# A seventh seven-product pair and a half piece per chunk in a hybrid encoder layer, with late keys and values parked in DRAM

## The chip, the cores and the metric

One core of one Trainium2 chip runs the kernel. Its engines each work through a queue of their own: TensorE (matmuls and weight loads), VectorE (elementwise), ScalarE (activations and copies), GpSimd, and SyncE, which issues the DMAs here. The metric is the device time of one execution in microseconds; the lower the better. The kernel before takes 1543.43 us, the median of three runs (1542.38 to 1543.45).

## The reference, cut to what matters

All data are float32. One layer on 256 tokens and 4096 features:

```python
h = layer_norm(x, emb_ln_g, emb_ln_b)              # (256, 4096)
p = h @ w_in                                       # w_in (4096, 13312)
c_b, c_c, c_h, c_z = four slices of 2048 columns   # convolution branch
a_q (2048), a_k (512), a_v (512), a_z (2048)       # attention: 16 query, 4 kv heads of 128
y_conv = c_b * conv3(c_c * c_h, conv_w) * silu(c_z)
y_attn = window_attention(a_q, a_k, a_v, sink) * silu(a_z)   # +-128 tokens, ALiBi, sink logit
y = concat(y_conv, y_attn) @ w_out                 # w_out (4096, 4096)
out = layer_norm(2 ** 0.25 * h + y, ln_g, ln_b)
```

Nearly all arithmetic is in the two matrix products, and nearly all bytes are their weights.

## The kernel before

**Tiling.** The 256 tokens are two blocks of 128 rows; the 4096 input features are 32 k-tiles of 128. The columns of w_in are cut into 26 chunks of 512, taken in the order of IN_ORDER: K, V, then AZ and Q alternately for four groups of four heads (AZ0, Q0, ... Q3), then CC, CH, CZ, CB four times (CC0 ... CB3). The output product follows in nine chunks.

**Split products.** Each float32 operand is used as a high and a low part, x = xh + xl and w = wh + wl, and each product as three matmuls: xh wh, xh wl, xl wh. xT holds the normalised input, turned, in both parts. The weights come from DRAM by SyncE into a raw buffer; ScalarE writes the high part (split_hi, L197), VectorE subtracts it for the low part (split_lo, L201).

**Steps.** The work is a written-out list of steps. A whole piece ("s" in ORDERS) is four k-tiles of a chunk, 1 MB, 24 matmuls of 512 columns (mm). A pair ("S") is two k-tiles, 512 KB, computed as a 2 x 2 block product (two halves of the tokens, two halves of the columns) with seven block products instead of eight: 21 matmuls of 256 columns (mm_pair). It needs sums of weight blocks (sums, L178 to L180, three VectorE operations that widen the 1024 loaded columns to 1792 to be split) and sums of input blocks, made once for each pair of k-tiles and kept in SC for all chunks (x_sums). x_sums also replaces a part of xT, so it runs after the last plain use of these k-tiles, which is in chunk V. K and V have eight whole pieces; the other 24 chunks have six pairs and five whole pieces. The pairs' results are gathered in PSUM in two more banks and put together by pair_copy and pair_sums (L649 to L652) and added by whole (L657).

**Order of the work.** The program order is the order of issue on each engine. Step j of the loop issues its matmuls, then split_hi of step j+3, then what `later` holds for j (the attention and convolution work, put at fixed distances from a chunk's end by `at`), then the loads that have a free buffer, then

```python
        loads(j)
        sums(j + 4)
        split_lo(j + 3)
```

The high and low parts have three buffers each, the raw weights three to six (w0 to w2, and w6 to w8 where memory is free). With four or more raw buffers a load is issued once the low part of the step that used the buffer, at most j+2, is issued; SyncE waits for it. During CC0's second half, CH0 and the start of CZ0 there are three.

**What `later` holds.** A chunk's end (chunk_end) is at the first step of the next chunk. After Q, the list SPREAD gives for four heads scores, s_add, exps, recip, norms, p_tr, p_lo, pv and out_z over 23 steps. After CH the product c * h is at the second step from there (L662), conv_tr at the fourth and fifth, conv_mul at the fifth and seventh; after CB the product with the gate, gate_tr and gate_mul at the same places. After AZ and CZ a SiLU is at the first step (z_act L504, s_act L691). In the first chunk's shadow K is turned into kT for four key heads (k_turn) and at V's end v is split (end_v); both stay in SBUF until the attention is done. y_load, y_hi and y_lo bring the finished branch outputs back as input of the output product during CB3 and the first output chunk.

Of the kernel before, what the change touches and what calls it, by code (L numbers as in the profile page):

```python
# [89 lines left out]
ALL_PAIRS = [u[1:] for u in IN_STEPS + OUT_STEPS if u[0] in ("pair", "opair")]  # L90
# [4 lines left out]
def encoder_kernel(ctx: ExitStack, tc: tile.TileContext, x, emb_g, emb_b, wi, ws, conv_w, sink, wo, ln_g, ln_b, out):  # L95
# [38 lines left out]
    def load(j, to=None):  # L134
# [47 lines left out]
    def part(j, t):  # L182
# [3 lines left out]
        return t[:, HW:] if is_pair(j) else t  # L186
# [38 lines left out]
    def mm(j):  # L225
# [4 lines left out]
        for k in range(PK):  # L230
            kt = q * PK + k
# [12 lines left out]
    def mm_pair(j):  # L244
# [10 lines left out]
        sc = lambda n: (SC[:, p, 0, n, :], SC[:, p, 1, n, :])  # L255
# [228 lines left out]
    kT = pa.tile([P, NG, 2, S], F32R, name="kT")  # L484
    v = pa.tile([P, 2, 2, W], F32R, name="v")
# [38 lines left out]
    def scores(h):  # L524
        g, a = h // GROUP, h % 2
# [565 lines left out]
```

## Time and profile before

| | us |
|---|---|
| median of three runs | 1543.43 |
| lowest, highest | 1542.38, 1543.45 |
| profiled execution | 1543.44 |
| its span in the profile | 1541.7 |
| TensorE busy with matmuls | 1525.8 |
| TensorE's weight loads, beside them | 1325.1 |
| VectorE busy | 1271.7 |
| ScalarE busy | 756.1 |

The span is from the first to the last instruction of the profiled execution; the time is that of the whole execution. Busy times of different engines overlap. The granted TensorE clock is at its full level in all 40 slices of the page. The DMAs moved 313.5 MB, 203 GB/s in the mean.

### The profile page before, as it was taken

The page shows a single profiled execution, that of the slowest core. Times are in us where ns is not written, and L with a number is a line of the kernel's source. Part 1 is how long each engine was busy: PE and PEld are TensorE (multiplying, and loading weights), DVE is VectorE, ACT ScalarE, POOL GpSimd, SP SyncE. Part 2 cuts the span into 40 slices and gives each one's busy share as a digit, 9 for nine tenths or more (in the row PEclk, how much of TensorE's full clock was granted, in tenths as well). Part 3 has the DMA queues.
Part 4 walks back from the last instruction along what each step waited for, and adds up shares of the span by engine and source line. Part 5 has one row for each costly group of instructions (what it writes and reads, how often), then busy time and mean ns, then how long its engine had stood idle before and what let it go on. Part 6 is the DMA issues. An engine that isn't in the chain of part 4 may idle for free.

```text
span 1541.7 us, 21128 instructions
## 1 busy us (share of the span) xinstructions
PE 1525.8 (99%) x8654; PEld 1325.1 (86%) x8654; DVE 1271.7 (82%) x1441; ACT 756.1 (49%) x640; POOL 1.3 (0%) x7
## 2 busy tenths in 40 slices
PE   7999999999999999999999999999999999999998
PEld 4888888888888888888888888888888888888897
DVE  7778798888897888898888889888888688888656
ACT  4545556556465554544544445444455444444331
POOL 0000000000000000000000000000000000000000
PEclk9999999999999999999999999999999999999999
DMA  7635554545545456656555655556557756666753
GB/s 283 223 138 203 205 191 169 196 175 182 203 158 188 164 188 238 217 191 208 194 199 191 219 205 186 187 208 218 192 188 274 276 185 225 253 203 235 252 182 140
DMA packets 67392, 313.51 MB, mean 203 GB/s; under 512 B 8064, under 2 KB 12128, under 8 KB 43488
## 3 DMA queue, kind: packets, MB, share of 16 engines
q1 hardware_dynamic: 66288, 310.33, 56.5%
q10 hardware_dynamic: 1008, 1.84, 0.3%
q8 instruction: 68, 1.11, 0.3%
q14 instruction: 28, 0.23, 0.0%
HBM read 304.19 MB, written 7.86 MB: 202 GB/s over the span
## 4 chain that ended last, share of the span: by engine, by line
PE 93%; DVE 3%; issue 2%; ACT 2%; DMA 0%; SPq 0%; ACTq 0%
PE acc L238 15%; PE acc L240 15%; PE acc L239 15%; PE acc L879 7%; PE acc L881 7%; PE acc L880 7%; PE pacc L263 5%; PE pacc L262 5%; PE pacc L264 4%; PE acc L263 3%; PE acc L262 3%; PE acc L264 3%; DVE wlo L201 1%; ACT whi L197 1%; PE att L476 1%
## 5 line engine op out<-in xcount | busy, mean ns | idle before, releaser
L197 ACT ACTIVATE whi<-w 128x2048 fp32r<-128x2048 f32 (+1 forms) x330 | 600.0, 1818 | 671.1 <-PE acc L240 292.3
L201 DVE TENSOR_TENSOR wlo<-w,whi 128x2048 fp32r<-128x2048 f32 (+1 forms) x330 | 712.1, 2164 | 200.1 <-ACT whi L197 198.3
L238 PE MATMUL acc<-whi,xT 128*128 128x512 f32 x1072 | 424.5, 396 | 0.0
L240 PE MATMUL acc<-whi,xT 128*128 128x512 f32 x1072 | 420.1, 392 | 0.0
L239 PE MATMUL acc<-wlo,xT 128*128 128x512 f32 x1072 | 417.4, 389 | 0.7 <-DVE wlo L201 0.7
L240 PEld LDWEIGHTS acc<-whi,xT 128*128 128x128 f32 x1072 | 201.3, 188 | 47.0
L239 PEld LDWEIGHTS acc<-wlo,xT 128*128 128x128 f32 x1072 | 201.3, 188 | 41.6 <-DVE wlo L201 1.0
L238 PEld LDWEIGHTS acc<-whi,xT 128*128 128x128 f32 x1072 | 201.5, 188 | 37.5
L879 PE MATMUL acc<-whi,xT 128*128 128x512 f32 (+1 forms) x496 | 182.9, 369 | 0.0
L881 PE MATMUL acc<-whi,xT 128*128 128x512 f32 (+1 forms) x496 | 181.8, 366 | 0.0
L880 PE MATMUL acc<-wlo,xT 128*128 128x512 f32 (+1 forms) x496 | 180.5, 364 | 0.0
L178 DVE TENSOR_TENSOR w<-w 128x512 f32<-128x512 f32 x154 | 105.2, 683 | 4.5 <-DMA w<-in_ws 4.5
L881 PEld LDWEIGHTS acc<-whi,xT 128*128 128x128 f32 x496 | 93.0, 188 | 16.9
L880 PEld LDWEIGHTS acc<-wlo,xT 128*128 128x128 f32 x496 | 93.1, 188 | 15.5
L879 PEld LDWEIGHTS acc<-whi,xT 128*128 128x128 f32 x496 | 93.2, 188 | 14.2 <-issue 0.4
L263 PE MATMUL acc<-wlo,xT 128*128 128x256 f32 x320 | 89.4, 279 | 0.0
L262 PE MATMUL acc<-whi,xT 128*128 128x256 f32 x320 | 89.3, 279 | 0.0
L264 PE MATMUL acc<-whi,xT 128*128 128x256 f32 x320 | 89.1, 279 | 0.0
L262 PE MATMUL pacc<-whi,xT 128*128 128x256 f32 x304 | 86.9, 286 | 0.0
L263 PE MATMUL pacc<-wlo,xT 128*128 128x256 f32 x304 | 84.9, 279 | 0.0
L264 PE MATMUL pacc<-whi,xT 128*128 128x256 f32 x304 | 84.7, 279 | 0.0
L263 PE MATMUL pacc<-wlo,SC 128*128 128x256 f32 x288 | 81.0, 281 | 0.0
(230 smaller groups left out, 1873.8 us busy)
## 6 DMA issues: line engine op xcount, KB each, us to landing
w<-in_wi SPq DMA_DIRECT2D x134, 1024.0 KB
w<-in_ws SPq DMA_DIRECT2D x154, 512.0 KB
w<-in_wo SPq DMA_DIRECT2D x43, 1024.0 KB
R<-in_wo SPq DMA_DIRECT2D x13, 1024.0 KB
x<-in_x SPq DMA_DIRECT2D x7, 512.0 KB
yl<-yd SPq DMA_DIRECT2D x7, 512.0 KB
xc<-in_x SPq DMA_DIRECT2D x14, 256.0 KB
R<-in_ws SPq DMA_DIRECT2D x6, 512.0 KB
```

Source lines behind the costliest of these rows:

```text
L178: nc.vector.tensor_tensor(s01, b22, b12.to_broadcast([P, 2, HW]), op=ALU.add)
L197: nc.scalar.activation(part(j, wh[j]), part(j, raw[j]), AF.Copy)
L201: nc.vector.tensor_tensor(part(j, wl[j]), part(j, raw[j]), part(j, wh[j]).bitcast(F32), op=ALU.subtract)
L238: nc.tensor.matmul(a, xh, hk, start=(first and k == 0), stop=False)
L239: nc.tensor.matmul(a, xh, lk, start=False, stop=False)
L240: nc.tensor.matmul(a, xl, hk, start=False, stop=(last and k == PK - 1))
L262: nc.tensor.matmul(o, ah, hi[:, w, :], start=(opens and p == 0), stop=False)
L263: nc.tensor.matmul(o, ah, lo[:, w, :], start=False, stop=False)
L264: nc.tensor.matmul(o, al, hi[:, w, :], start=False, stop=(closes and last))
L879: nc.tensor.matmul(o, yh, hk, start=first, stop=False)
L880: nc.tensor.matmul(o, yh, lk, start=False, stop=False)
L881: nc.tensor.matmul(o, yl, hk, start=False, stop=last)
```

## The change

NP goes from 6 to 7 in the 24 chunks with pairs, and their order from sSsSSsSsSSs to sSShSsSSsSSs: seven pairs, four whole pieces and one new half piece ("h", two k-tiles, 512 KB, 12 matmuls of 512 columns, mm with pk = 2, no sums of weights). A chunk has 12 steps where it had 11. The seventh x_sums runs in step 16, the first step of AZ0; the other six stay in steps 10 to 15. SC is two tiles, for five pairs and for two.

Room in SBUF: kT and v hold two head groups instead of four. k_turn and end_v make the parts of the last two groups in tiles that later hold pT and qhl and store them to DRAM (kd, vd). After the attention of groups 0 and 1, k_load and v_load (15 and 23 steps after Q's end) bring those of groups 2 and 3 into the places that have come free; the indices become h // GROUP % 2. end_v splits four half-width blocks where it split two. tab moves to the attention's pool. In the output product the residual's tile xc takes SC2's place, in the last chunk but one a part of z, which stands in SC's. The y_hi and y_lo entries from the tenth step on shift by one step where the chunk has become longer by one.

```diff
-NP = 6
+NP = 7
 PAIRS = [0, 0] + [NP] * (len(IN_ORDER) - 2)
-ORDERS = {0: "s" * 8, NP: "sSsSSsSsSSs"}
+ORDERS = {0: "s" * 8, NP: "sSShSsSSsSSs"}
...
-    q, p, us = 2 * PAIRS[ci] // PK, 0, []
+
+    q, p, us = -(-2 * PAIRS[ci] // PK), 0, []
     for u in ORDERS[PAIRS[ci]]:
         if u == "s":
             us.append(("in", ci, q))
             q += 1
+        elif u == "h":
+            us.append(("half", ci, PAIRS[ci]))
         else:
...
-        src = wi[IN_PIECES.index((a, b))] if kind == "in" else wo[OUT_PIECES.index((a, b))] if kind == "out" else None
+        src = {"in": (wi, IN_PIECES), "out": (wo, OUT_PIECES)}.get(kind, (ws, ALL_PAIRS))
+        src = src[0][src[1].index((a, b))]
...
-                nc.sync.dma_start(out=to[:, 0, :], in_=ws[ALL_PAIRS.index((a, b))])
+                nc.sync.dma_start(out=to[:, 0, :], in_=src)
...
-            nc.sync.dma_start(out=to, in_=src)
+            nc.sync.dma_start(out=to[:, 0:src.shape[1]], in_=src)
...
-        return t[:, HW:] if is_pair(j) else t
+        return t[:, HW:] if is_pair(j) else t[:, 0:4 * HW] if steps[j][0] == "half" else t
...
-        for k in range(PK):
-            kt = q * PK + k
+        pk, k0 = (2, 2 * q) if steps[j][0] == "half" else (PK, q * PK)
+        for k in range(pk):
+            kt = k0 + k
...
-    tab = const.tile([P, 2, S], F32, name="tab")
     ph, phs = ExitStack(), ExitStack()
     psc = ctx.enter_context(tc.tile_pool(name="psc", bufs=1))
-    SC = psc.tile([P, NP, 2, 3, HT], F32R, name="SC")
+    sc_tiles = [psc.tile([P, n, 2, 3, HT], F32R, name=name) for n, name in ((NP - 2, "SC"), (2, "SC2"))]
+    SC = [sc_tiles[p // (NP - 2)][:, p % (NP - 2), :, :, :] for p in range(NP)]
     pw = phs.enter_context(tc.tile_pool(name="pw", bufs=1))
     extra.append((pw, "w6"))
     pa = ph.enter_context(tc.tile_pool(name="pa", bufs=1))
+    tab = pa.tile([P, 2, S], F32, name="tab")
...
-    kT = pa.tile([P, NG, 2, S], F32R, name="kT")
-    v = pa.tile([P, 2, 2, W], F32R, name="v")
+    kT = pa.tile([P, 2, 2, S], F32R, name="kT")
+    v = pa.tile([P, 2, 2, 2, P], F32R, name="v")
+    kd = dram.tile([P, 2, 2, S], F32, name="kd")
+    vd = dram.tile([P, 2, 2, 2, P], F32, name="vd")
...
-        for b, ps in enumerate(turned(st_.pop("k"))):
-            halves(kT[:, 2 * b:2 * b + 2, 0, :], kT[:, 2 * b:2 * b + 2, 1, :], ps)
+
+        late = pa.tile([P, 2, 2, S], F32R, name="klate", tag="pT")
+        for t, ps in zip((kT, late), turned(st_.pop("k"))):
+            halves(t[:, :, 0, :], t[:, :, 1, :], ps)
+        nc.sync.dma_start(out=kd, in_=late.bitcast(F32))
 
     def end_v(ci, g):
+        late = pa.tile([P, 2, 2, 2, P], F32R, name="vlate", tag="qhl")
         for i in range(2):
-            halves(v[:, i, 0, :], v[:, i, 1, :], acc.pop((ci, i)))
+            ps = acc.pop((ci, i)).rearrange("p (a n) -> p a n", a=4)
+            halves(v[:, :, i, 0, :], v[:, :, i, 1, :], ps[:, 0:2, :])
+            halves(late[:, :, i, 0, :], late[:, :, i, 1, :], ps[:, 2:4, :])
+        nc.sync.dma_start(out=vd, in_=late.bitcast(F32))
+
+    def k_load(g):
+        nc.sync.dma_start(out=kT[:, g, :, :].bitcast(F32), in_=kd[:, g, :, :])
+
+    def v_load(g):
+        nc.sync.dma_start(out=v[:, g, :, :, :].bitcast(F32), in_=vd[:, g, :, :, :])
...
-        g, a = h // GROUP, h % 2
+        g, a = h // GROUP % 2, h % 2
...
-        t, g = st_.pop(("pT", h))[0], h // GROUP
+        t, g = st_.pop(("pT", h))[0], h // GROUP % 2
         o_ps = st_["o", h] = ps_att.tile([P, S], F32, name="att")
         for kb in range(2):
-            vh, vl = v[:, kb, 0, g * P:(g + 1) * P], v[:, kb, 1, g * P:(g + 1) * P]
+            vh, vl = v[:, g, kb, 0, :], v[:, g, kb, 1, :]
...
+            if g < 2:
+                at(j + 15, k_load, g)
+                at(j + 23, v_load, g)
...
+                    (9, y_load, 3), (10, y_hi, 2), (10, y_load, 4), (12, y_lo, 2), (12, y_hi, 3), (12, y_load, 5),
+                    (13, y_lo, 3), (13, y_hi, 4), (13, y_load, 6), (14, y_lo, 4), (14, y_hi, 5), (15, y_lo, 5),
+                    (15, y_hi, 6), (16, y_lo, 6), (16, y_hi, 7), (17, y_lo, 7)):
...
-        if ci == 1 and 2 <= q < 2 + NP:
-            x_sums(q - 2, pa.tile([P, 4 * S], F32, name="xs", tag="zT"))
+        if ci == 1 and q >= 2 or ci == 2 and j < NPC + 2 + NP:
+            x_sums(j - NPC - 2, pa.tile([P, 4 * S], F32, name="xs", tag="zT"))
...
-            xc = p2.tile([P, 2, w], F32, name="xc")
+        if n < ncs - 2:
+            xc = psc.tile([P, 2, w], F32, name="xc", tag="SC2")
+        elif n == ncs - 2:
+            zt.append(psc.tile([P, 8 * W], F32, name="z", tag="SC"))
+            xc = zt[0][:, 6 * W:6 * W + 2 * w].rearrange("p (a b) -> p a b", a=2)
         else:
-            z = psc.tile([P, NP * 2 * 3, HT], F32, name="z", tag="SC").rearrange("p a b -> p (a b)")
+            z = zt[0]
...
-            t = psc.tile([P, NP * 2 * 3, HT], F32R, name="SCy", tag="SC")
-            SC = t[:, 0:OP * 8, :].rearrange("p (k h s) t -> p k h s t", k=OP, h=2)
+            t = psc.tile([P, OP, 2, 4, HT], F32R, name="SCy", tag="SC")
+            SC = [t[:, p, :, :, :] for p in range(OP)]
...
-    ws = _np.stack([_np.stack([w_of(ci)[2 * p + k, :, h * HW:(h + 1) * HW] for k, h in ((0, 1), (1, 1), (0, 0), (1, 0))],
+    blocks = lambda half: ((0, 0), (0, 1), (1, 0), (1, 1)) if half else ((0, 1), (1, 1), (0, 0), (1, 0))
+    ws = _np.stack([_np.stack([w_of(ci)[2 * p + k, :, h * HW:(h + 1) * HW] for k, h in blocks(p == npairs(ci))],
```

Left out are the same edits for ALL_PAIRS (which takes the half pieces too), SC's two tiles in mm_pair and x_sums, and the y list as it was.

## Rows read from the trace of the kernel before

**Rows 1.** The page, part 1: busy time of each engine.
```profile
PE 1525.8 (99%) x8654; PEld 1325.1 (86%) x8654; DVE 1271.7 (82%) x1441; ACT 756.1 (49%) x640; POOL 1.3 (0%) x7
```

**Rows 2.** TensorE's waits: for whom, total us, times, longest us.
```profile
PE acc L239 <- DVE wlo L201: 0.7, 1, 0.7
```

**Rows 3.** Timeline of TensorE in CB0: start, us, line, tile.
```profile
629.47 0.40 PE L238 MATMUL acc<-whi,xT 128*128 128x512 f32 x1
...
634.97 0.28 PE L262 MATMUL pacc<-whi,xT 128*128 128x256 f32 x1
...
637.45 0.28 PE L262 MATMUL pacc<-whi,xT 128*128 128x256 f32 x1
...
639.92 0.40 PE L238 MATMUL acc<-whi,xT 128*128 128x512 f32 x1
```

**Rows 4.** Timeline of ScalarE in CB0.
```profile
629.72 1.70 ACT L197 ACTIVATE whi<-w 128x1792 fp32r<-128x1792 f32 x1 [0.77 <-PE pacc L264]
631.44 1.28 ACT L691 ACT_TABLE_LOAD   x1
632.73 1.06 ACT L691 ACTIVATE tm<-tm 128x1024 f32<-128x1024 f32 x1
635.22 1.92 ACT L197 ACTIVATE whi<-w 128x2048 fp32r<-128x2048 f32 x1 [1.43 <-issue]
```

**Rows 5.** Timeline of VectorE in CB0; in brackets the idle time before.
```profile
637.17 4.29 DVE L201 TENSOR_TENSOR wlo<-w,whi 128x2048 fp32r<-128x2048 f32 x2 [2.18 <-ACT whi L197]
641.38 0.69 DVE L178 TENSOR_TENSOR w<-w 128x512 f32<-128x512 f32 x1
...
642.90 2.28 DVE L201 TENSOR_TENSOR wlo<-w,whi 128x2048 fp32r<-128x2048 f32 x1
645.10 0.68 DVE L178 TENSOR_TENSOR w<-w 128x512 f32<-128x512 f32 x1
```

**Rows 6.** Timeline of VectorE in CZ0.
```profile
588.21 2.03 DVE L201 TENSOR_TENSOR wlo<-w,whi 128x1792 fp32r<-128x1792 f32 x1 [0.82 <-ACT whi L197]
590.15 1.22 DVE L662 TENSOR_TENSOR w<-w 128x1024 f32<-128x1024 f32 x1
591.29 0.69 DVE L178 TENSOR_TENSOR w<-w 128x512 f32<-128x512 f32 x1
...
599.51 0.69 DVE L178 TENSOR_TENSOR w<-w 128x512 f32<-128x512 f32 x1 [1.29 <-DMA w<-in_ws]
...
601.04 2.28 DVE L201 TENSOR_TENSOR wlo<-w,whi 128x2048 fp32r<-128x2048 f32 x1
```

**Rows 7.** Timeline of TensorE in CZ0, at a transpose.
```profile
602.63 0.60 PE L476 MATMUL att<-ident,w 128*128 128x128 f32 x4
602.98 0.36 PE L262 MATMUL pacc<-whi,xT 128*128 128x256 f32 x1
603.19 0.28 PE L263 MATMUL pacc<-wlo,xT 128*128 128x256 f32 x1
```

**Rows 8.** The chain of waits, in order of time, its longest pieces.
```profile
121.87 0.51 PE acc L239
```

**Rows 9.** Groups of ScalarE by line and shape: table loads.
```profile
L504 ACT ACT_TABLE_LOAD x4 | 5.1, 1283 | 0.1
...
L691 ACT ACT_TABLE_LOAD x1 | 1.3, 1283 | 0.0
```

**Rows 10.** Timeline of VectorE from V into AZ0.
```profile
108.84 0.69 DVE L613 TENSOR_TENSOR xs<-xT 128x512 f32<-128x512 f32 x1
...
111.85 2.02 DVE L201 TENSOR_TENSOR wlo<-w,whi 128x1792 fp32r<-128x1792 f32 x1
...
116.81 1.29 DVE L481 TENSOR_TENSOR v<-acc,v 128x512 fp32r<-128x512 f32 x2
...
119.53 2.29 DVE L201 TENSOR_TENSOR wlo<-w,whi 128x2048 fp32r<-128x2048 f32 x1
```

**Rows 11.** Timeline of SyncE's DMA issues in CZ0.
```profile
596.25 0.83 SPq L151 DMA_DIRECT2D w<-in_ws  x2
```

More of the change, by code (lines that the diff above doesn't have):

```diff
@@ L89 @@
 OUT_STEPS = [u for n in range(len(CHUNKS)) for u in out_units(n)]
-ALL_PAIRS = [u[1:] for u in IN_STEPS + OUT_STEPS if u[0] in ("pair", "opair")]
+ALL_PAIRS = [u[1:] for u in IN_STEPS + OUT_STEPS if u[0] in ("pair", "half", "opair")]
 OUT_PIECES = [u[1:] for u in OUT_STEPS if u[0] == "out"]
@@ L143, in load @@
                 to = raw[j] = pool.tile([P, PIECE], F32, name=name, bufs=1)
-        src = wi[IN_PIECES.index((a, b))] if kind == "in" else wo[OUT_PIECES.index((a, b))] if kind == "out" else None
+        src = {"in": (wi, IN_PIECES), "out": (wo, OUT_PIECES)}.get(kind, (ws, ALL_PAIRS))
+        src = src[0][src[1].index((a, b))]
         if len(to.shape) == 3:
             if is_pair(j):
-                nc.sync.dma_start(out=to[:, 0, :], in_=ws[ALL_PAIRS.index((a, b))])
+                nc.sync.dma_start(out=to[:, 0, :], in_=src)
             else:
                 nc.sync.dma_start(out=to, in_=src.rearrange("p (i n) -> p i n", i=2))
-        elif is_pair(j):
-            nc.sync.dma_start(out=to[:, 0:4 * HW], in_=ws[ALL_PAIRS.index((a, b))])
         else:
-            nc.sync.dma_start(out=to, in_=src)
+            nc.sync.dma_start(out=to[:, 0:src.shape[1]], in_=src)
     def loads(j):
@@ L254, in mm_pair @@
         x = lambda kt, i: (xT[:, kt, i * HT:(i + 1) * HT], xT[:, kt, (2 + i) * HT:(3 + i) * HT])
-        sc = lambda n: (SC[:, p, 0, n, :], SC[:, p, 1, n, :])
+        sc = lambda n: (SC[p][:, 0, n, :], SC[p][:, 1, n, :])
         p0, p1, c0, c1 = pacc[ci, 0], pacc[ci, 1], acc[ci, 0], acc[ci, 1]
@@ L618, in x_sums @@
             nc.vector.tensor_tensor(s[:, k, :], o0, o1, op=op)
-        if SC.shape[3] == 4:
-            return halves(SC[:, p, 0, :, :], SC[:, p, 1, :, :], s)
-        halves(SC[:, p, 0, :, :], SC[:, p, 1, :, :], s[:, 0:3, :])
+        if SC[p].shape[2] == 4:
+            return halves(SC[p][:, 0, :, :], SC[p][:, 1, :, :], s)
+        halves(SC[p][:, 0, :, :], SC[p][:, 1, :, :], s[:, 0:3, :])
         halves(x[:, 0, HT:2 * HT], x[:, 0, 3 * HT:4 * HT], s[:, 3, :])
@@ L762, in encoder_kernel @@
     for t, f, q in ((3, y_load, 0), (5, y_hi, 0), (6, y_lo, 0), (6, y_load, 1), (7, y_hi, 1), (8, y_lo, 1), (8, y_load, 2),
-                    (9, y_load, 3), (10, y_hi, 2), (10, y_load, 4), (11, y_lo, 2), (11, y_hi, 3), (11, y_load, 5),
-                    (12, y_lo, 3), (12, y_hi, 4), (12, y_load, 6), (13, y_lo, 4), (13, y_hi, 5), (14, y_lo, 5),
-                    (14, y_hi, 6), (15, y_lo, 6), (15, y_hi, 7), (16, y_lo, 7)):
+                    (9, y_load, 3), (10, y_hi, 2), (10, y_load, 4), (12, y_lo, 2), (12, y_hi, 3), (12, y_load, 5),
+                    (13, y_lo, 3), (13, y_hi, 4), (13, y_load, 6), (14, y_lo, 4), (14, y_hi, 5), (15, y_lo, 5),
+                    (15, y_hi, 6), (16, y_lo, 6), (16, y_hi, 7), (17, y_lo, 7)):
         at(last0 + t, f, q)
@@ L819, in encoder_kernel @@
     lnw = {}
-    first_cols = []
+    first_cols, zt = [], []
     def rows_load():
```

## The prediction

> **What bounds the kernel now.** I read the page's busy times first, then TensorE's waits, then the timelines of TensorE, ScalarE and VectorE over one chunk and over the passage from V to the first paired chunk. TensorE is busy 99% of the span, VectorE 82%, ScalarE 49% [rows 1]. In the whole run TensorE waits once for VectorE, 0.7 us for the low part of a weight piece [rows 2]. So time is gained by fewer matmul columns and lost wherever a low part comes later than TensorE reaches it.
>
> The pipeline has a fixed shape. The high part of step n is written into one of three buffers, so it starts when the matmuls of step n-3 have ended: the one at 629.72 starts 0.25 us after TensorE went on to the next step at 629.47, that at 635.22 0.25 us after 634.97 [rows 3, 4]. The low part follows on VectorE, behind whatever was issued there earlier, the sums of step n+1 among it. TensorE needs the low part only for its second matmul, 0.23 us into a whole piece (5.50 us in 24 matmuls).
>
> For a whole piece after two pairs this is near enough already. At 635.22 its high part begins, 1.92 us later its low part starts at 637.17, takes 2.29 us and ends at 639.46; TensorE starts that step at 639.92 and wants the low part at 640.15 [rows 3 to 5]. That leaves 0.69 us, with nothing ahead of it on VectorE.
>
> **Part 1, the seventh pair.** A whole piece of four k-tiles takes 634.97 - 629.47 = 5.50 us, a pair (two k-tiles) 2.475 us, the mean of 2.48 and 2.47 [rows 3]. Half a piece is 12 matmuls, 12 x 0.2293 = 2.75 us. So a seventh pair in place of two k-tiles saves 0.278 us a chunk; the half piece costs per k-tile what a whole one does. 24 chunks have pairs: -6.7 us. Rounded starts put this between -6.2 and -7.2.
> By the Trainium skill ("TensorE: Matmul & The Clock Gate", section "Back-to-back issue gap") a warm matmul of N columns costs N/2.4 + 2.5 ns, 216 ns at 512 and 109 ns at 256 columns. The rows have 229 and 118, so the trace differs; by that rule the saving would be an estimated 0.295 us a chunk, 7.1 us in all.
>
> VectorE pays: a pair needs 1.52 us of sums and a low part of 1792 columns, pitch 1.94, so 3.46 us in place of half of 2.20 us [rows 5, 6]; less what the half piece keeps, +2.4 us in a chunk of 42.1 us. At 82% on average it fits; what counts is order.
>
> **Part 2, the new order sSShSsSSsSSs.** I number the positions 0 to 11. The narrow place is the whole piece at 5, after pair (2), half (3), pair (4). Its low part stands behind the low part of 4 and the sums of 6. From TensorE's start of position 2: 0.25, the high part of 4 (1.71), 0.03, its low part (pitch 1.94), the sums of 6 (1.52), the low part of 5 (2.29): 7.74 us. TensorE gets there after 2.475 + 2.75 + 2.475 + 0.23 = 7.93. Room: 0.2 us, in place of 0.69. Everything else that stands in this stretch now delays TensorE.
>
> *The products.* In the chunks after a CH or CB chunk (four CZ, three CC) the element-wise product is issued at position 2, so behind the low part of 4: 590.15 to 591.29, 1.14 us [rows 6]. TensorE's own transposes at position 4 shift it by 0.36 us, 602.63 to 602.98, and stretch the next matmul a little, 0.09 us as I read 603.19 - 602.98 against 0.12 [rows 7]. 0.2 + 0.45 - 1.14 = -0.5 us. A stalled stream restarts 0.12 us slower: the matmul at 121.87, after the one wait, shows 0.51 us where 0.39 is usual [rows 8]. 7 x 0.6 = +4.2 us. Bounds: nothing (if the room is larger than I read) to 7 x 1.14 = 8.0.
>
> *SiLU with a table load.* At position 1 SiLU goes in front of the high part of 5. With its table load the row is 1.28 + 1.06 us and 0.15 to the next [rows 4]: the high part of 5 starts 4.48 us after position 2's start instead of 2.73, its low part ends at 4.48 + 1.92 + 0.03 + 2.29 = 8.72, 0.8 late, 0.9 with the restart. The load comes with SiLU five times [rows 9]. In Q1 to Q3 TensorE has scores and a value product (2 x 6 matmuls of 0.118 us, 1.4 us) between positions 2 and 5, which covers it; in Q0 and CB0 not. 2 x 0.9 = +1.8 us. Bounds: 0 to 5 x 0.9 = 4.5.
>
> Softmax work elsewhere adds to TensorE at least what it takes of room, 0.7 us of scores at position 4 against 0.6 us of VectorE's query remainder after the narrow place: 0, upper bound 3 us. CH and the later CB chunks have nothing at positions 1 and 2 but a SiLU of 1.06 us, hidden in the 1.52 us of sums: 0.
>
> **Part 3, the seventh x_sums.** V's steps are 8 to 15; x_sums ran in steps 10 to 15, and now once more in 16, the first of AZ0. One takes 108.84 to 111.85, 3.01 us of VectorE [rows 10]. Here VectorE is already late: it makes the low part of step 18 at 119.53 to 121.82, and that is the 0.7 us wait [rows 2, 8, 10]. With the new order step 18 is a pair, so its sums (1.52) go ahead of 111.85: low part of 17 from 113.37, x_sums from 115.31, V's parts from 118.32. V's four parts replace two that take 1.29 us together [rows 10]; as four operations I take 1.8 (bounds 1.3 and 2.4). Low part of 18: 120.1 to 122.1. TensorE came there at about 121.87 - 0.7 = 121.1: 1.0 us late. Step 18 ends at 124.5. Then x_sums to 125.05, sums of 20 to 126.6, and only then the low part of the half piece 19, whose duration no row shows: from 2.29 at 2048 and 2.03 at 1792 columns I take 1.23 us at 1024 (bounds 1.0 and 2.0), to 127.8. TensorE wants it at 124.7: 3.1 us late. Step 20's high part waits for the same sums: 126.8 to 128.5, low part 130.5, 0.1 late. Step 21's low part stands behind the sums of 22: 134.2 against 133.1, 1.1 late. From 22 on it is in time. Sum 5.3, four restarts 0.5, less the 0.8 that is there today: +5.0 us. Bounds: 2 (most of it hidden by work I have put too early) to 7.
>
> **Part 4, what I cost at nothing.** The stores of the late keys and values wait on SyncE's queue for VectorE's last part; the weight loads of that step stand behind them. The load for step 21 goes out about 6 us later, at 120.2; half a piece took at most 3.3 us from 596.25 to 599.51 [rows 6, 11], so a whole one is in by 126.8, and its high part starts only at 128.5. Without that cover: 2 us. k_load and v_load wait for scores and value products issued one step earlier, while the weight load behind them waits for a low part ending later; each is 256 KB, half of the 3.3 us transfer: 0 to 2 us for all four. The stretch with three weight buffers: the sums at 599.51 waited 1.29 us for their load, and the low part behind them started only after, at 601.04 [rows 6]. Positions 6 and 9 in CH0 have 2.7 to 3.4 us for such a load, but VectorE has room there: 0, upper bound 2. tab's place, the two SC tiles and the epilogue's tiles move bytes, not instructions; y_hi and y_lo keep their distance to the end of the input chunks. The two lists end alike (sSSs).
>
> **Sum.** -6.7 + 4.2 + 1.8 + 5.0 = +4.3 us on the profiled execution's 1543.44 us (span 1541.7, 1.7 around it), which is the median of the runs (1543.43): **1547.8 us**. I call 0.2%, 3.1 us, what can be told from no change: 1540.3 to 1546.5.
>
> **The rivals.**
> *Full gain.* VectorE averages 82% and TensorE waited once [rows 1, 2]; if the low parts keep up, 1543.4 - 6.7 = 1536.7, with some startup loss up to 1540. Against it is the 0.2 us of room. It decides if the product and SiLU no longer stand ahead of position 5. Chance 0.13.
> *Gain and startup cancel.* The steady chunks hold, x_sums costs 5: 1541.7; with part of the stalls up to 1546.5. For it: 0.5 us a product is close to my reading errors. 0.27.
> *VectorE or the loads become the bound more widely*, through three-buffer loads or softmax chunks: the upper bounds of parts 2 and 4 add 5 to 8 us, 1553 to 1556. 0.09.
> *Weight loading sets the pace.* A pair has 21 weight loads, two k-tiles of a piece 12. If loads ran end to end at the piece's pace of 0.229 us a matmul, a pair would take 4.8 us and the 24 new ones add 50 us: 1593. The pair's 2.475 us excludes it as it stands [rows 3]: 0.01. The Trainium skill ("Perfetto Trace Analysis", section "Identifying the Most-Contended Engine") would have TensorE's headroom judged by weight-load time, 86% here [rows 1].
> *Forecast*, startup and repeated stalls, 1545 to 1551, likeliest 1547.8: 0.50.
>
> Slower: 0.09 + 0.01 and 0.44 of the forecast, 0.54. Within 0.2%: 0.06 of the forecast (its low end lies under 1546.5) and the cancelling case, 0.33. Faster: 0.13. The range 1540 to 1552 leaves out most of full gain and the wide cases; the forecast's own is 1545 to 1551.
>
> **What would show it.** Right: TensorE waits for the low part in the chunk after V (one of about 3 us), in seven CC and CZ chunks at position 5 by 0.5 us, in Q0 and CB0 by 0.8; plain chunks 42.1 us, before 42.4. Wrong: no waits for low parts, or a long one named for a weight load. What would make it wrong is another order on VectorE than the one issued, or a half piece that costs more than 2.75 us.

## The result, and the profile after

The changed kernel takes 1549.87 us (median of 4 runs, 1549.09 to 1550.28) against 1542.91 us for the kernel before on the same chip: ratio 1.0043, 95% interval 1.0028 to 1.0058. The profiled execution took 1549.91 us with a span of 1548.2 us, 6.5 us longer than before.

The page's busy times answer to [rows 1], TensorE's waits (us in total, times, longest) to [rows 2]:

```profile
PE 1523.4 (98%) x8870; PEld 1330.6 (86%) x8870; DVE 1327.2 (86%) x1546; ACT 776.9 (50%) x668; POOL 1.3 (0%) x7
```
```profile
PE acc L242 <- DVE wlo L203: 6.8, 11, 2.8
PE pacc L266 <- DVE wlo L203: 1.7, 1, 1.7
PE acc L906 <- DVE w L203: 1.4, 1, 1.4
...
PE att L591 <- ACT p L584: 0.5, 3, 0.2
```

In the input chunks one wait for a low part has become twelve, 8.5 us in all (first two lines; the third is the last piece of the output product). TensorE saved its columns and spent them standing still. The table gives chunk times worked out from TensorE's timeline (start of a chunk's first matmul to that of the next chunk), for this kernel, the one before, and the experiments below. "Product" are CC1 to CC3 and CZ1 to CZ3, "plain" CH1 to CH3 and CB1 to CB3, "softmax" the eight chunks AZ1 to CH0.

| kernel | AZ0 | Q0 | softmax | CZ0 | CB0 | product, 6 | plain, 6 | all 24 |
|---|---|---|---|---|---|---|---|---|
| before | 43.33 | 43.24 | 378.17 | 43.95 | 42.36 | 259.44 | 254.16 | 1064.65 |
| changed | 48.80 | 43.71 | 377.32 | 44.33 | 42.72 | 262.01 | 252.33 | 1071.22 |
| parking only | 44.47 | 43.16 | 377.90 | 43.95 | 42.36 | 259.44 | 254.16 | 1065.44 |
| sums early | 46.09 | 43.84 | 377.66 | 44.34 | 42.73 | 261.95 | 252.31 | 1068.92 |
| product early | 49.02 | 43.95 | 377.67 | 43.83 | 42.76 | 257.72 | 252.29 | 1067.24 |
| SiLU late | 48.44 | 42.94 | 376.33 | 44.16 | 42.03 | 262.04 | 252.36 | 1068.30 |
| later turns | 48.72 | 43.59 | 373.37 | 43.70 | 42.73 | 262.03 | 252.35 | 1066.49 |
| piece first | 46.38 | 43.13 | 379.10 | 44.04 | 42.03 | 260.42 | 252.41 | 1067.51 |
| four moves | 45.86 | 43.08 | 376.20 | 44.55 | 42.03 | 257.71 | 252.31 | 1061.74 |
| all moves | 44.24 | 43.13 | 379.19 | 43.85 | 42.34 | 260.42 | 252.32 | 1065.49 |
| five moves | 42.06 | 44.00 | 373.54 | 42.97 | 42.06 | 257.70 | 252.30 | 1054.63 |
| before, five moves | 42.36 | 43.24 | 374.44 | 44.03 | 42.36 | 259.44 | 254.16 | 1060.03 |

A plain chunk fell by 0.305 us (254.16 to 252.33 over six), which is 7.3 us over 24. AZ0 alone is 5.5 us longer than before. VectorE's timeline at the start of AZ0, which answers to [rows 10]:

```profile
114.72 0.68 DVE L632 TENSOR_TENSOR xs<-xT 128x512 f32<-128x512 f32 x1
...
117.72 0.42 DVE L485 TENSOR_TENSOR v<-acc,v 128x256 fp32r<-128x256 f32 x1
118.59 0.43 DVE L485 TENSOR_TENSOR vlate<-acc,vlate 128x256 fp32r<-128x256 f32 x1 [0.45 <-ACT vlate L484]
118.94 0.41 DVE L485 TENSOR_TENSOR v<-acc,v 128x256 fp32r<-128x256 f32 x1
119.80 0.42 DVE L485 TENSOR_TENSOR vlate<-acc,vlate 128x256 fp32r<-128x256 f32 x1 [0.45 <-ACT vlate L484]
120.14 2.02 DVE L203 TENSOR_TENSOR wlo<-w,whi 128x1792 fp32r<-128x1792 f32 x1
122.08 0.69 DVE L632 TENSOR_TENSOR xs<-xT 128x512 f32<-128x512 f32 x1
...
126.62 1.22 DVE L203 TENSOR_TENSOR wlo<-w,whi 128x1024 fp32r<-128x1024 f32 x1
...
132.06 2.29 DVE L203 TENSOR_TENSOR wlo<-w,whi 128x2048 fp32r<-128x2048 f32 x1
```

The low parts of steps 18 and 19 come at 120.14 and 126.62, where the prediction put them (120.1 and 126.6); that this is luck is told below. V's four evictions take 2.42 us (117.72 to 120.14): VectorE stands idle 0.45 us twice, waiting for ScalarE's half. TensorE at step 19, and the granted clock (PEclk, the column before the last two) behind it:

```profile
124.68 0.40 PE L241 MATMUL acc<-whi,xT 128*128 128x512 f32 x1
127.89 0.79 PE L242 MATMUL acc<-wlo,xT 128*128 128x512 f32 x1 [2.81 <-DVE wlo L203]
128.48 0.63 PE L243 MATMUL acc<-whi,xT 128*128 128x512 f32 x1
128.91 0.63 PE L241 MATMUL acc<-whi,xT 128*128 128x512 f32 x1
```
```profile
124.60:128.00 3.40, 0.59 (x5) 0.26 (x3) 3.17 (x6) 1.13 (x1) 0.00 (x0) 0.92 0.67 267
128.00:130.00 2.00, 2.00 (x5) 1.61 (x6) 1.40 (x1) 2.00 (x2) 0.00 (x0) 0.50 0.54 164
130.00:132.00 2.00, 2.00 (x9) 1.59 (x9) 1.93 (x4) 0.37 (x1) 0.00 (x0) 0.79 0.42 131
```

After the 2.81 us wait the granted clock is 0.50, the lower level of 1.2 GHz, and a matmul starts every 0.43 us in place of 0.23, until about 131: step 19 takes 7.20 us where 2.755 + 2.98 (its second matmul at +3.21, not +0.23) is 5.73. So the lower clock cost this step another 1.5 us. Little of that is left at the chunk's end: the low part of step 21 ends only at 134.35 (132.06 + 2.29), and TensorE, late as it is, wants it at 134.56 and does not wait. Had it come 1.5 us earlier, it would have waited some 1.3 us there and restarted (an estimate from these rows).

### The profile page after: what moved, and what is told of

Same layout as the page of the kernel before. It is cut to its first block, busy times and chain, and to the rows that moved or that the text cites. A ratio compares the mean times of both kernels' runs of the same rounds, so it can differ in the third digit from the quotient of the medians.

```text
span 1548.2 us, 21816 instructions
## 1 busy us (share of the span) xinstructions
PE 1523.4 (98%) x8870; PEld 1330.6 (86%) x8870; DVE 1327.2 (86%) x1546; ACT 776.9 (50%) x668; POOL 1.3 (0%) x7
## 4 chain that ended last, share of the span: by engine, by line
PE 83%; DVE 8%; ACT 4%; issue 2%; DMA 2%; SPq 0%; ACTq 0%
PE acc L242 13%; PE acc L241 12%; PE acc L243 12%; PE acc L905 7%; PE acc L907 6%; PE acc L906 6%; DVE wlo L203 5%; PE pacc L266 4%; PE pacc L265 4%; PE pacc L267 4%; PE acc L266 3%; PE acc L265 3%; PE acc L267 3%; ACT whi L199 3%; DMA x<-in_x 1%
## 5 line engine op out<-in xcount | busy, mean ns | idle before, releaser
L199 ACT ACTIVATE whi<-w 128x1792 fp32r<-128x1792 f32 (+1 forms) x354 | 620.3, 1753 | 644.2 <-PE acc L243 243.7
L203 DVE TENSOR_TENSOR wlo<-w,whi 128x1792 fp32r<-128x1792 f32 (+1 forms) x354 | 735.6, 2081 | 139.6 <-ACT whi L199 138.9
L242 PE MATMUL acc<-wlo,xT 128*128 128x512 f32 x976 | 384.1, 394 | 6.8 <-DVE wlo L203 6.8
L241 PE MATMUL acc<-whi,xT 128*128 128x512 f32 x976 | 386.2, 396 | 0.0
L243 PE MATMUL acc<-whi,xT 128*128 128x512 f32 x976 | 382.2, 392 | 0.0
L242 PEld LDWEIGHTS acc<-wlo,xT 128*128 128x128 f32 x976 | 183.8, 188 | 46.5 <-DVE wlo L203 10.4
L243 PEld LDWEIGHTS acc<-whi,xT 128*128 128x128 f32 x976 | 183.7, 188 | 41.1
L241 PEld LDWEIGHTS acc<-whi,xT 128*128 128x128 f32 x976 | 183.8, 188 | 36.0
L180 DVE TENSOR_TENSOR w<-w 128x512 f32<-128x512 f32 x178 | 121.7, 684 | 4.9 <-DMA w<-in_ws 4.9
L907 PEld LDWEIGHTS acc<-whi,xT 128*128 128x128 f32 x496 | 93.1, 188 | 16.3
L906 PEld LDWEIGHTS acc<-wlo,xT 128*128 128x128 f32 x496 | 93.1, 188 | 15.7
L905 PEld LDWEIGHTS acc<-whi,xT 128*128 128x128 f32 x496 | 93.2, 188 | 14.7 <-issue 0.4
L265 PE MATMUL acc<-whi,xT 128*128 128x256 f32 x368 | 102.6, 279 | 0.0
L267 PE MATMUL acc<-whi,xT 128*128 128x256 f32 x368 | 102.5, 279 | 0.0
L265 PE MATMUL pacc<-whi,xT 128*128 128x256 f32 x352 | 100.3, 285 | 0.0
L267 PE MATMUL pacc<-whi,xT 128*128 128x256 f32 x352 | 98.1, 279 | 0.0
L266 PE MATMUL pacc<-wlo,SC 128*128 128x256 f32 x336 | 94.7, 282 | 0.0
```

The source lines that it names most:

```text
L180: nc.vector.tensor_tensor(s01, b22, b12.to_broadcast([P, 2, HW]), op=ALU.add)
L199: nc.scalar.activation(part(j, wh[j]), part(j, raw[j]), AF.Copy)
L203: nc.vector.tensor_tensor(part(j, wl[j]), part(j, raw[j]), part(j, wh[j]).bitcast(F32), op=ALU.subtract)
L241: nc.tensor.matmul(a, xh, hk, start=(first and k == 0), stop=False)
L242: nc.tensor.matmul(a, xh, lk, start=False, stop=False)
L243: nc.tensor.matmul(a, xl, hk, start=False, stop=(last and k == PK - 1))
```

## The experiments

The theory: the loss is the order in which VectorE and, ahead of it, ScalarE take their work. Rivals: the parking in DRAM, VectorE's sum of work, loads. Differences of a few tenths are read from the chunk table, because the output phase behind the input chunks varies by up to 2 us between kernels (last section).

**Parking only.** Six pairs and the old order in the changed kernel; all that is parked stays parked.
```
-NP = 7
+NP = 6
-ORDERS = {0: "s" * 8, NP: "sSShSsSSsSSs"}
+ORDERS = {0: "s" * 8, NP: "sSsSSsSsSSs"}
...
```
Left out is the old list of the y steps.


> The changed kernel with six seven-product pairs in each chunk, no half piece, the old step order sSsSSsSsSSs and the old list of the gated output's steps; the parking of two head groups' keys and values in DRAM, their loads back, and all moved tiles stay. VectorE-order theory: parking hides, because its stores and loads stand on SyncE and the two more evictions of V's accumulators end before a low part is late: 1543 us, within 2 of the kernel before, chunk AZ0 at 43.3 to 43.8 us. Rival (the parking's transfers or evictions make the loss): 1546 us or more, with chunk AZ0 or the softmax chunks as long as in the changed kernel (48.8, 47.6 us).


Measured: 1545.67 us, ratio 1.0017 [1.0008, 1.0026] to the kernel before. The transfers cost nothing that shows: no wait for a load, softmax chunks as before. But the evictions do: AZ0 is 1.14 us longer, where the prediction gave them 0.5 us. The four pieces stand on VectorE ahead of step 18's low part here too. Of the 2.1 us by which the span is longer, 1.5 us lie in the output phase. So both theories missed: parking is neither free nor the main loss.

**Sums early.** All seven operand sums beside V's pieces 1 to 7, none in AZ0.
```
-        if ci == 1 and q >= 2 or ci == 2 and j < NPC + 2 + NP:
-            x_sums(j - NPC - 2, ...)
+        if ci == 1 and q >= 1:
+            x_sums(q - 1, ...)
```


> The changed kernel with all seven operand sums made beside V's pieces 1 to 7 (one step earlier each), none in chunk AZ0. VectorE-order theory: chunk AZ0 falls from 48.8 to 43.0 to 43.6 us, everything else as it was: 1544.4 us (5.5 less than 1549.9). Rival (the parked copies' evictions, or seven sums as such, make VectorE late there): the same work is only moved ahead by 5.5 us, so chunk AZ0 stays above 46 us or chunk V grows from 44.8 us by what AZ0 loses.


Measured: 1548.74 us (ratio 1.0039 [1.0024, 1.0054]), AZ0 46.09 us: 2.7 us less, half of what I expected. Step 19 no longer waits; step 18 still loses 2.0 us behind V's evictions, and step 21, at position 5, 1.8 us. VectorE has won no lead: V's evictions begin 5.5 us into AZ0, as in the changed kernel, because a sum, a low part and the waits for ScalarE between them fill the 5.5 us of each step beside V. The seventh sum is half of the startup loss, not all of it.

**Product early.** One step earlier.
```
-                at(j + 2, product, key, other)
+                at(j + 1, product, key, other)
```


> The changed kernel with the product of the gate one step earlier, at the second step of its chunk and not the third. VectorE-order theory: VectorE is idle for some 1.2 us ahead of the low part of position 4, so the product fits there, the low part of position 5 comes 1.1 us earlier, and the seven chunks CC1 to CC3 and CZ0 to CZ3 fall from 43.62 to 44.33 us to about 42.1 to 42.9 us: 1545 us (4.9 less). Rival (the half piece or the two pairs in a row at positions 1 and 2 make these chunks longer, and the product is hidden): no change, 1549.9 us; second rival (no room at the second step either, the wait moves to position 4): the seven chunks stay within 0.3 us.


Measured: 1545.60 us, ratio 1.0014 [1.0005, 1.0023]; the six product chunks together 4.3 us less, CZ0 0.5 us: 4.8 us of the expected 4.9. All 24 chunks fell by 4.0 us, since AZ0, Q0 and the softmax chunks, which the move does not touch, are 0.8 us longer in this run. VectorE's timeline in CC1, first of the changed kernel, then of this one:
```profile
679.06 2.03 DVE L203 TENSOR_TENSOR wlo<-w,whi 128x1792 fp32r<-128x1792 f32 x1 [1.07 <-ACT whi L199]
681.00 1.22 DVE L681 TENSOR_TENSOR ug<-ug,tm 128x1024 f32<-128x1024 f32 x1
682.13 0.69 DVE L180 TENSOR_TENSOR w<-w 128x512 f32<-128x512 f32 x1
```
```profile
677.66 1.22 DVE L203 TENSOR_TENSOR wlo<-w,whi 128x1024 fp32r<-128x1024 f32 x1
678.80 1.22 DVE L681 TENSOR_TENSOR ug<-ug,tm 128x1024 f32<-128x1024 f32 x1
679.97 2.03 DVE L203 TENSOR_TENSOR wlo<-w,whi 128x1792 fp32r<-128x1792 f32 x1
```
In the first VectorE idles 1.07 us, waiting for position 4's high part, and then makes the product where it is in the way. In the second the product fills the hole. The work is the same.

**SiLU late.** One step later, behind the high part of position 5.
```
-            at(j + 1, s_act)
+            at(j + 2, s_act)
-            at(j + 1, z_act)
+            at(j + 2, z_act)
```


> The changed kernel with both kinds of SiLU one step later, at the third step of their chunk, so that on ScalarE they stand behind the high part of position 5 and not ahead of it. VectorE-order theory: Q0 (43.71 us) and CB0 (42.72 us), where the SiLU and its table load now stand ahead of that high part, fall by 0.6 to 0.75 us each, to some 43.0 and 42.07 us; the other chunks stay: 1548.5 us (1.4 less). Rival (ScalarE's time is hidden, VectorE alone sets the step): both chunks within 0.1 us, 1549.9 us. If the high part of position 6 then comes late, Q0 and CB0 lose at position 6 or 7 what they win at 5.


Measured: 1547.18 us, ratio 1.0028 [1.0016, 1.0041]. Q0 0.77 and CB0 0.69 us less, as expected. ScalarE's timeline in CB0, changed kernel first, answers to [rows 4]:
```profile
634.60 1.70 ACT L199 ACTIVATE whi<-w 128x1792 fp32r<-128x1792 f32 x1 [1.41 <-PE pacc L267]
636.32 1.28 ACT L710 ACT_TABLE_LOAD   x1
637.62 1.07 ACT L710 ACTIVATE tm<-tm 128x1024 f32<-128x1024 f32 x1
638.58 3.49 ACT L199 ACTIVATE whi<-w 128x2048 fp32r<-128x2048 f32 x2
```
```profile
632.34 1.70 ACT L199 ACTIVATE whi<-w 128x1792 fp32r<-128x1792 f32 x1 [1.41 <-PE pacc L267]
634.81 1.92 ACT L199 ACTIVATE whi<-w 128x2048 fp32r<-128x2048 f32 x1 [0.77 <-PE pacc L267]
636.75 1.28 ACT L710 ACT_TABLE_LOAD   x1
```
Not expected: Q1 to Q3 are 0.4 us shorter too, all of it at position 7, where TensorE turns head 3's probabilities. The way leads over VectorE: the high part ahead of head 3's exponentials waits for VectorE's sums (L182), which stand behind the low part of position 5. In Q1 it starts 20.13 us behind the chunk's start and not 20.84, and the normalisations 28.53 and not 28.92.

**Later turns.** Two of a group's four heads turn their probabilities a step later.
```
-    ... head(0, 4, 5, 6, 7, 8, 9, 10, 12, 13) ... 3, 14, 15, 16, 17, 18, 19, 20, 22, 23)
+    ... head(0, 4, 5, 6, 7, 8, 10, 11, 12, 13) ... 3, 14, 15, 16, 17, 18, 20, 21, 22, 23)
```


> The changed kernel with two of the four heads' probabilities turned one step later (head 0 at step 10 of its spread and not 9, head 3 at step 20 and not 19, their low parts at 11 and 21). VectorE-order theory, widened to ScalarE's order: in the two shortest positions TensorE's transposes of the probabilities wait up to 0.5 us for ScalarE's normalisation; with a step more they don't, and the pairs of softmax chunks (AZ and Q, 94.5 us together) fall by 0.3 to 0.4 us: 1548.5 us (1.0 to 1.4 less). Rival (the softmax chunks lose what they lose through the order of the transposes among the steps, not through a wait): no change within 0.5 us.


Measured: 1546.46 us, ratio 1.0027 [1.0018, 1.0036]; the softmax chunks 3.95 us less in all, about three times what I expected. TensorE's timeline in Q1, changed kernel and then this one:
```profile
279.86 0.28 PE L267 MATMUL pacc<-whi,SC 128*128 128x256 f32 x1
280.31 0.94 PE L591 MATMUL att<-ident,p 128*128 128x128 f32 x4 [0.17 <-ACT p L584]
281.01 0.48 PE L241 MATMUL acc<-whi,xT 128*128 128x512 f32 x1
```
```profile
285.50 0.60 PE L591 MATMUL att<-ident,p 128*128 128x128 f32 x4
285.85 0.36 PE L265 MATMUL pacc<-whi,xT 128*128 128x256 f32 x1
```
The view of waits names 0.17 us; from the last matmul's start to the next piece it is 1.15 us, and 0.35 from the first transpose's start with the probabilities ready. It counts idle time only from the modelled end of the matmul before (279.86 + 0.28). ScalarE's two normalisations end at 280.25 and 280.65, and a transpose starts 0.05 us behind each, at 280.31 and 280.71: it is a wait, twice, and not only another order of the transposes.

**Piece first.** Nothing but another order.
```
-ORDERS = {0: "s" * 8, NP: "sSShSsSSsSSs"}
+ORDERS = {0: "s" * 8, NP: "sSsSShSSsSSs"}
```


> The changed kernel, nothing but the step order altered: sSsSShSSsSSs, with the second whole piece at position 2 and the half piece at position 5, so that no two pairs follow each other at once and no whole piece stands at position 5. All seven products, sums, products of the gate and SiLUs stay where they are. VectorE-order theory: the low part of the piece at position 2 stands behind one pair's low part and no sums of a later pair, and at position 5 there is now a low part of half the size, so the seven chunks with the product fall to 42.95 us (4.9 us in all), Q0 and CB0 to 42.95 and 42.05 us (1.4 us), AZ0 to about 46 to 47 us: 1541 to 1543 us. Rival (a chunk with seven pairs has no room for the product in any order, VectorE's sum of work being the limit): the seven chunks stay at 43.6 us with the stall at position 8 in place of 5, and 1549 us or more.


Measured: 1546.60 us, ratio 1.0021 [1.0011, 1.0030], too little. CC1 to CC3 are at 42.95 us, Q0 at 43.13, CB0 at 42.03, AZ0 at 46.38, as expected: in those the product and the SiLU are hidden where they stand, so seven pairs have room for them. CZ1 to CZ3 are not (43.85 us): the convolution's products on VectorE now stand ahead of the piece at position 8, 0.8 us late. And Q1 to Q3 grow by 0.4 to 0.5 us, since head 3's turn waits longer. Each order has its own narrow place.

**Four moves.** Product early, SiLU late, the sums one step earlier still (pairs 0 and 1 beside V's piece 1, none beside piece 7), and V's evictions at AZ0's position 8:
```
+        for p in ((0, 1) if q == 1 else (q,) if 2 <= q < NP else ()) if ci == 1 else ():
+            x_sums(p, ...)
...
-            else:
+            elif ci == 1:
+                at(j + 9, chunk_end, j + 9, ci)
```


> The changed kernel in its own step order with four kinds of work moved: the operand sums of pairs 0 and 1 beside V's piece 1 and those of pairs 2 to 6 beside V's pieces 2 to 6, none beside piece 7 or in chunk AZ0; the evictions of V's accumulators nine steps later (in AZ0, behind the high part of its last piece); the product one step earlier; both SiLUs one step later. VectorE-order theory: AZ0 at 43.0 to 43.7 us (5.1 to 5.8 less), the seven chunks with the product at 42.95 us (4.8 less), Q0 at 43.0 and CB0 at 42.05 us, the other Q chunks at 47.2 us (2.9 less in all): 1536.5 to 1538 us, faster than the kernel before by 5 us. Rival (loads and TensorE's own restarts take part of it back, since every step then comes earlier by up to 13 us while the weights arrive at their old pace): over 1540 us with waits for weights in the trace.


Measured: 1538.32 us, ratio 0.9969 [0.9956, 0.9982]: faster than the kernel before. AZ0 runs without a wait up to its last piece and there loses 3.8 us, my own misplacement (a part of it is the lower clock, see the last section):
```profile
144.05 1.92 ACT L199 ACTIVATE whi<-w 128x2048 fp32r<-128x2048 f32 x1 [2.79 <-PE acc L243]
145.87 0.36 ACT L484 ACTIVATE v<-acc 128x256 fp32r<-128x256 f32 x1
```
```profile
139.29 4.02 DVE L203 TENSOR_TENSOR wlo<-w,whi 128x1792 fp32r<-128x1792 f32 x2
146.26 0.42 DVE L485 TENSOR_TENSOR v<-acc,v 128x256 fp32r<-128x256 f32 x1 [2.95 <-ACT v L484]
```
ScalarE's eviction stood behind a high part that waited for TensorE, and VectorE waited 2.95 us for it.

**All moves.** The four moves and the order of "piece first".

> The four moves and the step order sSsSShSSsSSs together. VectorE-order theory: once nothing waits for VectorE, the order of the steps gives nothing more: within 1 us of the kernel with the four moves alone, 1536 to 1538 us. Rival (the order moves the transposes to steps in which they cost TensorE more or less): the softmax chunks differ by 0.3 us or more from those of the kernel with the four moves.


Measured: 1545.88 us, ratio 1.0013 [0.9997, 1.0028]: 3.75 us more in the 24 chunks than the four moves alone (the medians are 7.6 us apart). My expectation fell and the rival held, with 3.0 us more in the softmax chunks: the order brings back the waits in CZ1 to CZ3 and Q1 to Q3.

**Five moves.** The four and the later turns, V's evictions one step earlier than in those (`j + 8`), and the same on the kernel before (`j + 7`).

> The changed kernel in its own step order with all moves that helped alone: the operand sums of pairs 0 and 1 beside V's piece 1 and of pairs 2 to 6 beside its pieces 2 to 6; the evictions of V's accumulators eight steps later, at AZ0's step 7, so that on ScalarE they stand ahead of the high part of AZ0's last piece (with the four moves they stood behind it, and VectorE waited 2.95 us for them); the product one step earlier; both SiLUs one step later; head 0's and head 3's probabilities turned one step later. VectorE-order theory: AZ0 43.0 us (2.8 less than with the four moves), the softmax chunks 0.2 to 0.5 us less each: 1538.3 less 2.8 less 2.5 is 1533 us. Rival (the loads bind once all comes earlier, above all in CZ0, where three weight buffers are left): 1535 us or more, CZ0 above 44.6 us.

> The kernel before with the same five moves (six pairs, its own step order; V's evictions seven steps later). It tells whether the moves are worth their time by themselves or only undo what the change brought. VectorE-order theory: the kernel before stalls only for 0.7 us in AZ0 and 0.3 to 0.8 us in each of the AZ and Q chunks for the turned probabilities, the product and the SiLU being hidden there: 1542.9 less 1 less 3 to 4 is 1538.5 to 1540 us, some 5 to 6 us above the changed kernel with the moves. Rival (the moves help both kernels alike): the two kernels differ by 2 us or less.


Measured: 1535.09 us, ratio 0.9945 [0.9931, 0.9958], the fastest of all; the kernel before with the same moves 1538.78 us, 0.9969 [0.9958, 0.9980]. TensorE's waits that are left in the changed one's input chunks:
```profile
PE acc L242 <- DVE wlo L203: 1.0, 2, 0.6
```
One is at Q0's position 5, for a reason that was not tried, and one at CH0's position 8. There VectorE itself waited for a load, in the stretch with three weight buffers, and the low part followed these sums:
```profile
550.70 0.69 DVE L180 TENSOR_TENSOR w<-w 128x512 f32<-128x512 f32 x1 [1.08 <-DMA w<-in_ws]
```
So the rival, that the loads bind, holds in one place, though not in CZ0, where it was to show above all (42.97 us). In 24 chunks the two kernels differ by 5.4 us, and without the excess of these two places (0.9 us over Q0 with the four moves, 0.7 us over Q1 to Q3) by 7.0 us: nearly TensorE's whole saving of 7.3. In medians 3.7 us are left, where I expected 5 to 6: with the same moves in both kernels that is what the change is worth. To the kernel before the moves are worth 4.9 us by themselves (1543.70 to 1538.78).

**Room.** Spare additions on VectorE at position 2 of the plain chunks: one in CH1 and CB1, two in CH2 and CB2, three in CH3 and CB3.
```
...
+            nc.vector.tensor_tensor(spare, x0, x0, op=ALU.add)
...
```


> The changed kernel with spare additions of 128x256 on VectorE (0.42 us each, their result used by nothing) at the third step of chunks that have no product there: one in CH1 and CB1, two in CH2 and CB2, three in CH3 and CB3. It measures the room of the whole piece at position 5, 0.2 us by the prediction's step. VectorE-order theory: one addition makes the chunk 0.22 to 0.3 us longer, two 0.64 to 0.75 us, three 1.06 to 1.2 us, all of it a wait for the low part at position 5; 4 to 4.5 us in all, about 1554 us. Rival (VectorE's 14% of idle time takes up such work): one and two additions cost nothing, three less than 0.5 us; second rival (no room at all): 0.42, 0.84 and 1.26 us.


Measured: 1553.51 us (a single run; 1543.74 us for the kernel before beside it). The chunks are longer by 0.29 and 0.36 us, 0.78 and 0.78, 1.21 and 1.22. CH1, VectorE without and with one addition:
```profile
722.68 2.03 DVE L203 TENSOR_TENSOR wlo<-w,whi 128x1792 fp32r<-128x1792 f32 x1 [1.17 <-ACT whi L199]
724.62 0.68 DVE L180 TENSOR_TENSOR w<-w 128x512 f32<-128x512 f32 x1
...
726.14 2.28 DVE L203 TENSOR_TENSOR wlo<-w,whi 128x2048 fp32r<-128x2048 f32 x1
```
```profile
722.43 2.03 DVE L203 TENSOR_TENSOR wlo<-w,whi 128x1792 fp32r<-128x1792 f32 x1 [1.19 <-ACT whi L199]
724.38 0.42 DVE L794 TENSOR_TENSOR spare<-xT 128x256 f32<-128x256 f32 x1
724.71 0.68 DVE L180 TENSOR_TENSOR w<-w 128x512 f32<-128x512 f32 x1
...
726.23 2.28 DVE L203 TENSOR_TENSOR wlo<-w,whi 128x2048 fp32r<-128x2048 f32 x1
```
From the start of position 4's low part to that of position 5's it is 3.46 and 3.80 us: the addition moves it by 0.34. TensorE's second matmul at position 5 stood at +0.24 and is now at +0.42, 0.18 us late: the room is 0.16 us (0.2 predicted). The chunk is 0.29 us longer, so the restart costs 0.11 (0.12 predicted). VectorE is idle 14% of the span, and work at this place still costs nearly its whole duration.

## Why the prediction was right, point by point

The direction, the place and the mechanism held; the total, +6.5 us where +4.3 was forecast, is off by the sizes of several terms, and two terms that were set to nothing cost something.

- **TensorE's saving**, -6.7 predicted, -7.3 measured (24 x 0.305, from the plain chunks); with nearly all in its place the two kernels differ by 7.0 us. By the Trainium skill ("TensorE: Matmul & The Clock Gate", section "Back-to-back issue gap") an estimated 7.1 us was given (0.298 us a chunk; the 0.295 is a slip). The section gives its 216 ns at 512 columns for a matmul by itself, and about 131 ns in a stream with weight loads. These matmuls, each with its weight load, start every 229 ns, and every 118 ns at 256 columns, where the rule has 109: its sum agrees with the trace, its terms do not.
- **The narrow place at position 5**: right. 0.16 us of room and 0.11 us for a restart, shown by the additions.
- **Products**, +4.2 predicted, +4.8 shown by moving them.
- **SiLU with a table load**, +1.8 predicted, +1.5 shown in Q0 and CB0. Costed at nothing in Q1 to Q3, it cost 0.4 us in each: not at position 5, as feared there, but by making head 3's probabilities late on ScalarE, at position 7.
- **The startup**, +5.0 predicted. AZ0 lost 5.5 us and its saving of 0.3: 5.8. The term of the sum that was mis-sized is V's four evictions: 2.42 us, and not 1.8. This does not show in the clock times, because AZ0 begins 0.6 us earlier in this profile than in the one before (112.22 and 112.82). Counted from AZ0's start, V's evictions begin where the sum has them and everything behind them on VectorE is 0.6 us later; that the low parts of steps 18 and 19 came at the forecast times is luck, two differences of 0.6 us that cancel. Step 18 lost 2.0 us and not 1.0 through these 0.6 us and because I took TensorE's arrival 0.2 us too late: the wait of the kernel before was 0.85 us from its due time (step 18 began at 120.79), not 0.7. The 1.1 us at step 21 did not come; the lower clock at step 19, which the sum did not have, came in its place. In "SiLU late", where AZ0 has the same instructions, the lower clock fell into the end of step 18 (0.50 in 124 to 126), step 21 did lose 1.15 us, and AZ0 took 48.44 us, not much less than 48.80. Sums early and parking only show what the startup is made of: 2.7 us the seventh sum, 1.1 us the two more evictions; that the remaining 2.0 us are the order with its two pairs in a row is argued from piece first (2.4 us less), which changes more than that.
- **Softmax**, 0 predicted (bound 3). The saving of eight chunks is 2.4 us and the chunks fell by 0.85, which is 1.6 short. Of these, 0.7 us is no loss: with 12 steps to a chunk, step 22 of SPREAD falls at the end of the second chunk and no longer into the chunk behind it, so the last group's value product for head 3 has gone from CZ0 to CH0 (six matmuls, the first one before and after):
```profile
583.05 0.28 PE L586 MATMUL att<-pT,v 128*128 128x256 f32 x1
```
```profile
575.84 0.28 PE L605 MATMUL att<-pT,v 128*128 128x256 f32 x1
```
  The other 0.9 us is about what SiLU late wins in these chunks (1.0 us), so it is in the main the SiLU of Q1 to Q3 once more. This term failed: I weighed VectorE's query remainder against TensorE's scores and did not follow ScalarE's normalisations to the transposes that wait for them. Later turns win 3.95 us; most of this is no cost of the change, since the kernel before had such waits too and wins 3.7 us in these chunks by all five moves.
- **Three weight buffers**, 0 predicted (bound 2). CZ0 loses some 0.6 us more at position 8 than CZ1. Behind a load that VectorE waited for, it had no pause up to that low part:
```profile
599.41 0.69 DVE L180 TENSOR_TENSOR w<-w 128x512 f32<-128x512 f32 x1 [0.52 <-DMA w<-in_ws]
```
- **Parking, epilogue**: the transfers are hidden, as predicted. From the end of the input chunks on the span is some 0.5 us longer than before. The last low part of the output product came 1.4 us late for TensorE (third row of the waits above), but TensorE was early: the load of its weights went out 40.3 us before the span's end in both kernels, and the eighth output chunk took 21.76 us where it had taken 22.61. Whether the epilogue's tiles had a part in it was not tried.

These terms add up: -7.3 + 4.8 + 1.5 + 5.8 + 0.9 + 0.6 = +6.3 us in the 24 chunks, where the table has 6.6; with 0.5 behind them and 0.6 less ahead of V, where TensorE's first wait was shorter in this execution, the span is 6.5 us longer. Without those 0.6 us the miss would be larger.

The rivals. "Full gain", 1536.7 us, is not what five moves show, though they reach 1535.1 us: 4.9 us of that the kernel before wins by the same moves, and beside it the change gains 3.7 us in medians and 5.4 us in the 24 chunks. It does come near in the chunks, under the condition named for it, that the product and the SiLU no longer stand ahead of position 5, and with the startup and the turns mended as well. "Gain and startup cancel" fell: the steady chunks did not hold. "VectorE as such is the bound" is ruled out: the same work, elsewhere, nearly does not show. "Weight loading sets the pace" is ruled out too: with a pair more in each of 24 chunks the weight loads went from 1325.1 to 1330.6 us, and the plain chunks became shorter.

## What to carry to other kernels

When a change takes work from the engine that bounds a kernel and gives it to one that is 80 to 90% busy, the average says little: find the step with the least room, write down in issue order what stands ahead of its last input on each in-order queue, and move that work by one step into a hole. A step can be too early as well as too late: an eviction issued behind something that waits for TensorE holds up the other engine that needs it. Follow every engine's queue to every consumer, too: here the normalisations ahead of turned probabilities, set to nothing, cost 0.9 us, and the evictions in turn, set to 0.5 us, cost 1.1. Last, compare a changed kernel with the old one after both have had the same repairs: more than half of what the five moves won was there to be won without the change.

## What the runs showed of the hardware

The same wait can cost the clock or not. In the four moves' kernel TensorE stood 1.88 us at AZ0's last piece, the granted clock was 0.78 in 151 to 153 and 0.50 in 153 to 155, and the step took 9.28 us; with all moves it stood 1.88 us at the same piece with no such loss (7.67 us). In AZ0 of the changed kernel and of "SiLU late", the same instructions, TensorE stood 1.74 us at step 18 in both; the granted clock was 1.00 in 122 to 126 in the one and 0.50 in 124 to 126 in the other:
```profile
124.00:126.00 2.00, 2.00 (x11) 2.00 (x11) 1.52 (x4) 0.62 (x2) 0.00 (x0) 0.50 0.94 360
```
Why is open.

At the granted clock of 1.00 TensorE has two paces. The windows of two whole pieces in the changed kernel, in V and in AZ0 behind its waits (us, then TensorE busy, weight loads, VectorE, ScalarE, GpSimd, granted clock):
```profile
101.24:106.73 5.49, 5.49 (x25) 4.51 (x24) 4.48 (x12) 2.53 (x3) 0.00 (x0) 1.00 0.28 96
144.88:150.48 5.60, 5.60 (x27) 4.54 (x26) 4.93 (x5) 1.70 (x1) 0.00 (x0) 1.00 0.80 279
```
24 matmuls start every 229 ns in the one and every 233 ns in the other. The slower pace follows some waits, not all (in "later turns" the pieces behind the same waits took 5.49 us), and holds for several steps. It occurs in the output phase as well: in "parking only" the eight pieces of the seventh output chunk took 44.80 us, before 43.95. This and the loads of the chunk ahead of it (42.9 to 44.2 us) are part of why the medians of two kernels can differ by 1 to 2 us from their input chunks. What sets the pace was not tried.

Two engines that empty one accumulator in turn wait for each other: ScalarE and VectorE took 2.42 us for four pieces of 256 columns, with 0.45 us idle on VectorE twice, against 1.29 us for two of 512 [rows 10].
